# Constants on TensorE ahead of the first loads, the first pair in order of arrival, and the x casts and w_down sums at other places

## The chip, the cores and the metric

The kernel runs on one core of a Trainium2 chip. The time is the device time of one execution in microseconds (us), given as the median of several executions. Stage times inside an execution come from the trace of one profiled execution, counted from the start of its span; the span is about 2 us shorter than the device time (2303.0 for 2304.98 in before).

## The reference, cut to what matters

A gated MLP with 8 x 1024 tokens, hidden size 1024 and intermediate size 4096, all in float32:

```python
gate = x @ w_gate                      # x: (8, 1024, 1024), w_gate, w_up: (1024, 4096)
up = x @ w_up
gate = 0.5 * gate * (1 + np.tanh(np.sqrt(2 / np.pi) * (gate + 0.044715 * gate ** 3)))
h = gate * up
return (h @ w_down).astype(np.float32) # w_down: (4096, 1024)
```

## The kernel before

Eight passes of 1024 tokens. Each has a gate/up phase, which makes h, and a down phase, which multiplies h by w_down. All products are in float16 and use sums of blocks of the operands so that there are fewer products than blocks: seven for eight in passes 0 to 2. There one "pair" of 128-column blocks of gate and up takes 14 products of 4 matmuls; 16 pairs make a gate/up phase. Products are numbered 1 to 14 inside a pair, and other work is hung behind a product's number, which sets its place among the instructions of its engine.

Three inputs are prepared beside this. **x of the next pass** is cast to float16 by a transfer from DRAM to DRAM that GpSimd issues (`cast_x`), and then transposed by four transfers in the sync engine's queue (`transpose_x`). **Raw weights** come by casting loads that GpSimd issues (`load_raw`), and VectorE makes their sums (`sum_w`). **w_down** is loaded in pass 0 in four blocks, summed by VectorE and stored (`wd_load`, `wd_sums`, `wd_store`); the down phases read it back in chunks (`load_d`).

```python
def cast_x(p):
    r = slice(p * TOK, (p + 1) * TOK)
    nc.gpsimd.dma_start(out=xh[r, :], in_=x2[r, :])
...
# pass 0, block n of w_down: (distance from product s0, what, arguments)
s0 = 28 * n + 59
for ds, f, a in (
    (0, wd_load, (n, 0)), (2, wd_load, (n, 1)),
    (4, wd_load, (n, 2)), (6, wd_load, (n, 3)),
    (16, wd_sums, (0,)), (17, wd_sums, (1,)),
    (18, wd_sums, (2,)), (19, wd_sums, (3,)), (21, wd_store, (n,)),
):
    pr, k = divmod(s0 + ds - 1, 14)
    if pr == i:
        at(k + 1, f, *a)
...
if i == 4 and p == FAST - 1:           # FAST = 3: x of pass 3 in pair 4 of pass 2
    at(2, cast_x, p + 1)
...
# down phase, first product group
if v == 0 and p < FAST - 1:            # x of passes 1 and 2
    cast_x(p + 1)
if v == (2 if p < FAST - 1 else 0):
    transpose_x(p + 1)
```

In a pair from the third on, the ends of the products are used like this. "add s2 0" frees a PSUM bank, and in the next pair the ScalarE copies of the first product's sum ("copy 0", "copy 1") stand behind the gelu of that sum:

```python
AFTER1 = {
    1: ["copy 0"],                     # ScalarE: PSUM bank to PSUM bank
    2: ["copy 1"],
    ...
    11: ["h21"],                       # VectorE: up times gelu(gate)
    12: ["h11"],
    13: ["add s2 0"],                  # VectorE; its gelu is issued after product 1 of the next pair
    14: ["add s2 1"],
}
```

The first pair is special: x and the first weights come in pieces, and x is transposed on TensorE.

```python
def first_pair():                      # shortened
    for g in range(G): x0_cast(0, g)                   # VectorE, waits for the loads of x
    for g in range(G): x0_transpose(0, g)              # 8 transposes, one copy each by VectorE and ScalarE
    for kh in range(2):
        for w in range(2): cast_first(w, kh, slice(0, 256))    # ScalarE
    for kh in range(2): products(0, kh, slice(0, MH))  # 32 matmuls of 512 columns
    for g in range(2): x0_cast(1, g)
    for g in range(2): x0_transpose(1, g)
    outputs(0, 0); outputs(0, 1)                       # gelu and product
    for g in range(2, G): x0_cast(1, g)
    for kh in range(2): products(1, kh, slice(0, MQ))  # 32 of 256 columns
    for g in range(2, G): x0_transpose(1, g)
    for n, (kh, w) in enumerate(((0, 0), (0, 1), (1, 0), (1, 1))):
        cast_first(w, kh, slice(256, 512))
        if n == 1:                                     # trigger: waits for this cast
            nc.gpsimd.tensor_copy(mark, raw(0, 0)[:, w, kh * KH, 256:257])
            load_raw(0, 1)                             # second block of weights
    for kh in range(2): products(1, kh, slice(MQ, MH))
    ...
```

Of the kernel before, what the change touches and what calls it, by code (L numbers as in the profile page):

```python
# [14 lines left out]
GELU = mybir.ActivationFunctionType.Gelu_apprx_tanh  # L15
# [84 lines left out]
def kernel(  # L100
# [8 lines left out]
    nc = tc.nc  # L109
    x2 = x.flatten_outer_dims()  # L110
    out2 = out.flatten_outer_dims()
    P = 128
# [4 lines left out]
    MH = 512  # L117
# [6 lines left out]
    G = MH // P  # L124
# [94 lines left out]
    def x0_cast(mh, g):  # L219
        nc.vector.tensor_scalar(x0_f16[:, mh * G + g], x0_f32[mh][:, g], XSC, None, MUL)  # L220

    def x0_transpose(mh, g):
        h = x0_f16[:, mh * G + g]
        b = ps_free.popleft()
        ps = ps_all[:, b].bitcast(FP16).rearrange("p (k m) -> p k m", m=P)
        for k in range(2 * KH):
            nc.tensor.transpose(ps[:, k], h[:, k * P : (k + 1) * P], identity)
        c = slice(g * P, (g + 1) * P)
        nc.vector.tensor_copy(xq["b11" if mh == 0 else "b12"][:, :, c], ps[:, 0:KH])
        nc.scalar.copy(xq["b21" if mh == 0 else "b22"][:, :, c], ps[:, KH : 2 * KH])  # L230
        ps_free.append(b)


    def raw(p, q):
# [292 lines left out]
    def gate_up_one(p):  # L527
        for i in range(NP):
            q, e = divmod(i, 2)
            extra = {k: [] for k in range(1, 15)}  # L530

            def at(k, f, *a):
                extra[k].append(lambda: f(*a))

            if p == 0 and i == 0:
                first_pair()
                continue
            if p == 0:
                if e == 1:
                    at(13, load_raw, p, q + 2)  # L540
                if 11 <= i < 15:
                    at(7, half_load, 0, 2 * (i - 11))
                if i >= 14:
                    at(4, half_load, 1, 4 * (i - 14))
                    at(6, half_load, 1, 4 * (i - 14) + 2)
                for n in range(4):

                    s0 = 28 * n + 59
                    for ds, f, a in (
                        (0, wd_load, (n, 0)), (2, wd_load, (n, 1)),  # L550
                        (4, wd_load, (n, 2)), (6, wd_load, (n, 3)),
                        (16, wd_sums, (0,)), (17, wd_sums, (1,)),
                        (18, wd_sums, (2,)), (19, wd_sums, (3,)), (21, wd_store, (n,)),
                    ):
                        pr, k = divmod(s0 + ds - 1, 14)
                        if pr == i:
                            at(k + 1, f, *a)
            elif i == 0:
                at(1, load_raw, p, 1)
            elif e == 1:  # L560

                at(13, load_raw, p, q + 2)

            ks = (3, 5, 7, 9) if e == 0 else (11, 12, 13, 14)
            for n, k in enumerate(ks):
                at(k, sum_w, p, i + 1, n)

            if FAST - 2 <= p < FAST:
                for j, n in enumerate(entries_of(p - FAST + 2)):
                    if j // 6 == e:  # L570
                        at(2 * (j % 6) + 2, make_entry, p, q, n)
            if i == 4 and p == FAST - 1:
                at(2, cast_x, p + 1)
            if i == NP - 2:
                order[0] = [0, 1, 4, 2, 3, 5] if p % 2 == 0 else [2, 3, 4, 0, 1, 5]
                if p:
                    at(2, load_d, p, 0)
                    at(3, load_d, p, 1)
            if i == NP - 1:
                at(1, load_d, p, 2 if p else 0)  # L580
            second = p == 0 and i == 1
            pair(p, i, extra, SEQ0 if second else SEQ, AFTER0 if second else AFTER1)
# [134 lines left out]
    def down(p):  # L717
# [65 lines left out]
        for v, name in enumerate(DSEQ):  # L783
# [3 lines left out]
            for nb in range(2):  # L787
                kc = 2 * v + nb
                dc = d_chunk(p, kc)
                for g in range(G):  # L790
# [43 lines left out]
                            f()  # L834
                    if nb == 0 and g == 0 and p + 1 < NPASS:

                        if v == 0 and p < FAST - 1:
                            cast_x(p + 1)
                        if v == (2 if p < FAST - 1 else 0):
                            transpose_x(p + 1)  # L840
# [29 lines left out]


    def first_pair():
        bank = {}

        def products(mh, kh, c):
            for w in range(2):
                for j in range(2):
                    for k in range(KH):
                        nc.tensor.matmul(  # L879
                            ps_all[:, bank[mh, j, w], c],  # L880
                            raw(0, 0)[:, w, kh * KH + k, j * P : (j + 1) * P],
                            xq[f"b{kh + 1}{mh + 1}"][:, k, c],
                            start=(kh == 0 and k == 0 and c.start == 0),
                            stop=(kh == 1 and k == KH - 1),
                            skip_group_check=True,
                        )

        def outputs(mh, j):
            t = tmp_free.popleft()
            g, u = bank[mh, j, 0], bank[mh, j, 1]  # L890
            nc.scalar.activation(tmp[:, t], ps_all[:, g], GELU, scale=GSC)
            nc.vector.tensor_tensor(
                hq[f"a{mh + 1}{j + 1}"][:, 0, :], ps_all[:, u], tmp[:, t], MUL
            )
            tmp_free.append(t)
            ps_free.extend((g, u))

        def take(mh):
            for j in range(2):
                for w in range(2):  # L900
                    bank[mh, j, w] = ps_free.popleft()

        for g in range(G):
            x0_cast(0, g)
        for g in range(G):
            x0_transpose(0, g)
        for kh in range(2):
            for w in range(2):
                cast_first(w, kh, slice(0, 256))
        take(0)  # L910
        for kh in range(2):
            products(0, kh, slice(0, MH))
        for g in range(2):
            x0_cast(1, g)
        for g in range(2):
            x0_transpose(1, g)
        outputs(0, 0)
        outputs(0, 1)
        for g in range(2, G):
            x0_cast(1, g)  # L920
        take(1)
        for kh in range(2):
            products(1, kh, slice(0, MQ))
        for g in range(2, G):
            x0_transpose(1, g)

        b = list(ps_free)
        ps_free.clear()
        ps_free.extend((b[2], b[0], b[3], b[1]))
        for n, (kh, w) in enumerate(((0, 0), (0, 1), (1, 0), (1, 1))):  # L930
            cast_first(w, kh, slice(256, 512))
            if n == 1:

                nc.gpsimd.tensor_copy(mark, raw(0, 0)[:, w, kh * KH, 256:257])
                load_raw(0, 1)
        for kh in range(2):
            products(1, kh, slice(MQ, MH))
        sum_x(1)
        sum_w(0, 1, 0)
        sum_w(0, 1, 1)  # L940
        sum_x(2)
        outputs(1, 0)
        outputs(1, 1)
        sum_x(3)
        sum_w(0, 1, 2)
        sum_w(0, 1, 3)
        sum_x(4)
# [46 lines left out]
```

## Time and profile before

| | us |
|---|---|
| time before, median of 3 (lowest to highest) | 2301.93 (2298.45 to 2304.24) |
| start until the second pair's first product | 33.53 |
| pass 0, gate/up from there | 187.11 |
| pass 0, down | 102.47 |
| pass 1, gate/up and down | 194.13 and 96.69 |
| pass 2, gate/up | 196.81 |
| everything after that | 1492.26 |

These stages are read off TensorE's timeline of the profiled execution (span 2303.0): a stage begins where its first product starts. A down phase with no wait takes 96.69; pass 0's takes 5.78 more. 15 pairs of 12.09 us are 181.4; pass 0 takes 5.8 more. What the start, the three gate/up phases and that down phase have above their matmuls at full clock is what a change like this one can win.

The chain of work that ended last says the same in one line, as shares of the span by engine: most of the chain is TensorE itself, and some 8% goes through transfers and VectorE.

```profile
PE 90%; DMA 5%; DVE 3%; issue 1%; ACT 1%; POOL 0%; SPq 0%; POOLq 0%; DVEq 0%; ACTq 0%
```

Three stretches of 3.4 us, the time that the clock stayed at half after it fell (294.70 to 298.11): the two ahead of the place where TensorE's clock rose (18.22), and the one ahead of the place where it fell. The columns are the stretch, its length, then for TensorE matmuls, TensorE loads, VectorE, ScalarE and GpSimd the busy us and the count, then the granted clock, the DMA share and GB/s (the clock reads 1.00 in the first two lines too, ahead of the trace's first record of a change; there the count of matmuls, 14 in 5.80 us, shows the half clock):

```profile
11.40:14.80 3.40, 2.42 (x6) 0.88 (x7) 0.00 (x0) 3.32 (x4) 0.00 (x0) 1.00 1.10 375
14.80:18.20 3.40, 3.40 (x9) 1.21 (x8) 1.39 (x2) 0.53 (x1) 0.00 (x0) 1.00 1.02 408
291.30:294.70 3.40, 0.89 (x5) 0.45 (x6) 2.34 (x4) 0.00 (x0) 0.00 (x0) 1.00 1.01 357
```

Behind the first stretch, with 2.42 us of matmuls, the next is still slow: 9 matmuls in 3.40 us. After the second, in which TensorE was busy for all 3.40 us, they run at 216 ns. In the third, which holds most of the long wait, TensorE was busy for 0.89 us, and the following 3.4 us ran at half clock.

### The profile page before, as it was taken

The page shows a single profiled execution, that of the slowest core. Times are in us where ns is not written, and L with a number is a line of the kernel's source. Part 1 is how long each engine was busy: PE and PEld are TensorE (multiplying, and loading weights), DVE is VectorE, ACT ScalarE, POOL GpSimd, SP SyncE. Part 2 cuts the span into 40 slices and gives each one's busy share as a digit, 9 for nine tenths or more (in the row PEclk, how much of TensorE's full clock was granted, in tenths as well). Part 3 has the DMA queues.
Part 4 walks back from the last instruction along what each step waited for, and adds up shares of the span by engine and source line. Part 5 has one row for each costly group of instructions (what it writes and reads, how often), then busy time and mean ns, then how long its engine had stood idle before and what let it go on. Part 6 is the DMA issues. An engine that isn't in the chain of part 4 may idle for free.

```text
span 2303.0 us, 38141 instructions
## 1 busy us (share of the span) xinstructions
PE 2277.2 (99%) x14696; PEld 1436.5 (62%) x14696; DVE 1348.0 (59%) x1945; ACT 958.4 (42%) x1860; POOL 670.1 (29%) x818
## 2 busy tenths in 40 slices
PE   7999999999999999999999999999999999999999
PEld 4444444444444445888468874788747886488854
DVE  5566348873487753667446673476734667256650
ACT  4444125551255512555135551355414653055520
POOL 1333003320133300545014540254403543034520
PEclk9999999999999999999999999999999999999999
DMA  8898968989799876988679885798858988588852
GB/s 213 148 214 191 232 199 203 222 240 287 177 213 232 239 262 227 289 305 278 200 257 308 287 269 199 261 318 277 269 197 269 311 283 265 187 280 279 269 213 109
DMA packets 258054, 557.20 MB, mean 242 GB/s; under 512 B 74768, under 2 KB 134160, under 8 KB 243728
## 3 DMA queue, kind: packets, MB, share of 16 engines
q1 hardware_dynamic: 204992, 483.46, 62.4%
q0 software_dynamic: 52880, 71.31, 18.8%
q8 instruction: 115, 1.88, 0.3%
q14 instruction: 67, 0.55, 0.1%
HBM read 512.75 MB, written 113.25 MB: 272 GB/s over the span
## 4 chain that ended last, share of the span: by engine, by line
PE 90%; DMA 5%; DVE 3%; issue 1%; ACT 1%; POOL 0%; SPq 0%; POOLq 0%; DVEq 0%; ACTq 0%
PE ps L683 39%; PE ps L795 33%; PE ps L476 17%; DMA ring<-in_w_up_dram 2%; DMA h_s<-in_w_down_dram 2%; DVE ring L275 1%; DVE tmp L495 1%; DMA ring<-wd_ops 0%; PE ps L879 0%; DMA w_ops<-x_sums 0%; DVE h_a L513 0%; DMA h_a<-in_x_dram 0%; DVE x_sums L201 0%; POOL h_s L318 0%; ACT ring L253 0%
## 5 line engine op out<-in xcount | busy, mean ns | idle before, releaser
L683 PEld LDWEIGHTS <-ring 128*128 128x128 f16 x8320 | 813.7, 98 | 95.6
L660 POOL TENSOR_TENSOR h_a<-tmp 128x256 f16<-128x256 f32 x640 | 464.5, 745 | 928.3 <-ACT tmp L648 894.4
L683 PE MATMUL ps<-x_sums,ring 128*128 128x256 f16 x5760 | 655.8, 273 | 0.0
L795 PE MATMUL ps<-ring,h_a 128*128 128x512 f16 x2944 | 640.0, 380 | 3.9 <-DMA ring<-wd_ops 3.9
L645 DVE TENSOR_TENSOR tmp<-tmp,ps 128x512 f32<-128x512 f32 x640 | 413.7, 683 | 220.6 <-PE ps L683 167.8
L795 PEld LDWEIGHTS <-h_a 128*128 128x128 f16 x3072 | 300.7, 98 | 367.0 <-DVE x_b L183 4.4
L476 PEld LDWEIGHTS <-ring 128*128 128x128 f16 x2632 | 257.0, 98 | 320.8 <-issue 9.9
L630 ACT COPY tmp<-ps 128x512 f32<-128x512 f32 x520 | 304.1, 585 | 204.2 <-PE ps L683 121.9
L476 PE MATMUL ps<-x_sums,ring 128*128 128x512 f16 x1504 | 341.4, 379 | 7.5 <-DVE tmp L495 7.1
L648 ACT ACTIVATE tmp<-tmp 128x256 f32<-128x256 f32 x640 | 263.7, 417 | 173.0 <-DVE tmp L643 80.2
L734 ACT ACTIVATE tmp<-ps 128x512 f32<-128x512 f32 x128 | 76.4, 597 | 593.0 <-PE ps L795 591.9
L683 PE MATMUL ps<-x_b,ring 128*128 128x256 f16 x2560 | 305.6, 273 | 0.0
L476 PE MATMUL ps<-x_b,ring 128*128 128x512 f16 x1128 | 259.5, 379 | 0.5 <-ACT ps L492 0.5
L502 POOL TENSOR_TENSOR h_a<-tmp 128x512 f16<-128x512 f32 x94 | 145.3, 1546 | 382.6 <-ACT tmp L500 270.8
L643 DVE TENSOR_TENSOR tmp<-ps,tmp 128x512 f32<-128x512 f32 x240 | 165.3, 689 | 151.3 <-ACT tmp L630 105.2
L738 DVE SCALAR_TENSOR_TENSOR tmp<-ps,tmp 128x512 f32<-128x512 f32 x64 | 44.2, 690 | 309.2 <-ACT tmp L734 260.3
L495 DVE TENSOR_TENSOR tmp<-ps,tmp 128x512 f32<-128x512 f32 x188 | 126.9, 682 | 109.8 <-ACT tmp L487 106.8
L487 ACT COPY tmp<-ps 128x512 f32<-128x512 f32 x188 | 109.9, 585 | 91.7 <-PE ps L476 87.7
L742 DVE TENSOR_TENSOR h_a<-h_a,h_a 128x2048 f16<-128x2048 f16 x96 | 111.2, 1214 | 58.6 <-PE ps L795 58.6
L275 DVE TENSOR_TENSOR ring<-ring 128x1024 f16<-128x1024 f16 x188 | 135.0, 733 | 15.8 <-DMA ring<-in_w_up_dram 8.5
L500 ACT ACTIVATE tmp<-tmp 128x512 f32<-128x512 f32 x94 | 58.9, 626 | 153.4 <-DVE tmp L495 153.2
L795 PE MATMUL ps<-ring,h_s 128*128 128x512 f16 x480 | 104.9, 379 | 0.0
(65 smaller groups left out, 798.6 us busy)
## 6 DMA issues: line engine op xcount, KB each, us to landing
ring<-w_ops SPq DMA_DIRECT2D x480, 512.0 KB, 4.6
ring<-wd_ops SPq DMA_DIRECT2D x105, 1024.0 KB, 5.2
out_dram<-tmp SPq DMA_DIRECT2D x128, 256.0 KB, 2.5
w_ops<-x_sums SPq DMA_DIRECT2D x110, 256.0 KB, 6.5
ring<-in_w_gate_dram POOLq DMA_DIRECT2D x23, 1024.0 KB, 9.9
ring<-in_w_up_dram POOLq DMA_DIRECT2D x23, 1024.0 KB, 18.4
w_ops<-h_s SPq DMA_DIRECT2D x82, 256.0 KB, 5.5
x_half<-in_x_dram POOLq DMA_DIRECT2D x7, 2048.0 KB, 15.4
```

Of the source, the lines that this page charges most:

```text
L275: nc.vector.tensor_tensor(o, a, b, op)
L476: nc.tensor.matmul(ps(b, w), lhs[:, k], rhs[:, k, :], start=(first and k == 0), stop=(k == KH - 1), skip_group_check=True,)
L495: nc.vector.tensor_tensor(o, ps("b", w), o, ADD)
L502: nc.gpsimd.tensor_tensor(hq[TO[n]][:, i, :], tmp[:, t[n, 1]], tmp[:, t[n, 0]], MUL)
L630: nc.scalar.copy(tmp[:, t[o[1]]], ps_all[:, bank[o[2]]])
L643: nc.vector.tensor_tensor(d, b, a, SUB)
L645: nc.vector.tensor_tensor(d, a, b, ADD if o[4] == "add" else SUB)
L648: nc.scalar.activation(d, d, GELU, scale=GSC)
L660: nc.gpsimd.tensor_tensor(h, tmp[:, t[o[1]], MQ : 2 * MQ], g, MUL)
L683: nc.tensor.matmul(ps_all[:, bank[c], w * MQ : (w + 1) * MQ], lhs[:, w, k], rhs[:, k], start=(first and w == 0 and k == 0), stop=(k == KH ...
L742: nc.vector.tensor_tensor(hq[o][:, s, :], hq[a][:, s, :], hq[b][:, s, :], op)
L795: nc.tensor.matmul(ps_all[:, bank[b, g]], lhs[:, j, g * P : (g + 1) * P], dc[:, n, :], start=(first and j == 0), stop=(j == NP - 1), skip_ ...
```

## The change

Six things, none of which takes a product away:

- a. TensorE multiplies constants until the first products, and the gelu table is loaded at the start.
- b. The first pair's casts, gelus and products are issued in the order in which their inputs arrive.
- c. The second block of weights is loaded as soon as the second of the last four pieces of the first has come, not after ScalarE has cast that piece.
- d. The w_down sums of pass 0 stand 5 products later, and the store 4.
- e. x of pass 1 is cast in pair 2 of pass 0's gate/up phase, not in its down phase.
- f. x of pass 3 is cast in pair 13 of pass 2, not in pair 4.

```diff
-                        (16, wd_sums, (0,)), (17, wd_sums, (1,)),
-                        (18, wd_sums, (2,)), (19, wd_sums, (3,)), (21, wd_store, (n,)),
+                        (21, wd_sums, (0,)), (22, wd_sums, (1,)),
+                        (23, wd_sums, (2,)), (24, wd_sums, (3,)), (25, wd_store, (n,)),
...
-            if i == 4 and p == FAST - 1:
-                at(2, cast_x, p + 1)
+            if (p, i) in ((0, 2), (FAST - 1, 13)):
+                at(8, cast_x, p + 1)
...
-                        if v == 0 and p < FAST - 1:
+                        if v == 0 and 0 < p < FAST - 1:
                             cast_x(p + 1)
...
+        def warm(n):
+            for _ in range(n):
+                nc.tensor.matmul(ps_all[:, 0], warm_w, warm_x, start=True, stop=True)
+
+        warm_w, warm_x = hf["s3"][:, 0:P], hf["s3"][:, P : P + MH]
+        nc.vector.memset(hf["s3"][:, 0 : P + MH], 1.0)
+        nc.scalar.activation(mark, hf["s3"][:, 0:1], GELU)
         for g in range(G):
             x0_cast(0, g)
+        warm(9)
         for g in range(G):
-            x0_transpose(0, g)
+            x0_transpose(0, g, 4 + g)
+            warm(2 if g < G - 1 else 8)
...
         for g in range(2):
-            x0_transpose(1, g)
-        outputs(0, 0)
-        outputs(0, 1)
+            x0_transpose(1, g, 6 + g)
         for g in range(2, G):
             x0_cast(1, g)
-        take(1)
+        outputs(0, 0)
+        for w in range(2):
+            cast_first(w, 0, slice(256, 512))
+        nc.gpsimd.tensor_copy(mark, staging0(1, 0)[:, 0, 256:257])
+        load_raw(0, 1)
         for kh in range(2):
             products(1, kh, slice(0, MQ))
         for g in range(2, G):
-            x0_transpose(1, g)
-        ... (the four casts with the trigger behind the second)
+            x0_transpose(1, g, g - 2)
+        outputs(0, 1)
+        for w in range(2):
+            cast_first(w, 1, slice(256, 512))
         for kh in range(2):
             products(1, kh, slice(MQ, MH))
... (the banks of the first pair are given by number, no longer from the list of free ones)
```

Line numbers fall by one or two: L476, L495 and L275 of before are L474, L493 and L273 of the changed kernel, L879 is L877.

More of the change, by code (lines that the diff above doesn't have):

```diff
@@ L220, in x0_cast, with x0_transpose @@
         nc.vector.tensor_scalar(x0_f16[:, mh * G + g], x0_f32[mh][:, g], XSC, None, MUL)
-    def x0_transpose(mh, g):
+    def x0_transpose(mh, g, b):
         h = x0_f16[:, mh * G + g]
-        b = ps_free.popleft()
         ps = ps_all[:, b].bitcast(FP16).rearrange("p (k m) -> p k m", m=P)
@@ L230, in x0_transpose @@
         nc.scalar.copy(xq["b21" if mh == 0 else "b22"][:, :, c], ps[:, KH : 2 * KH])
-        ps_free.append(b)
     def raw(p, q):
@@ L872, in first_pair @@
     def first_pair():
-        bank = {}
+        bank = {(mh, j, w): 4 * mh + 2 * j + w for mh in range(2) for j in range(2) for w in range(2)}
         def products(mh, kh, c):
@@ L895, in outputs @@
             tmp_free.append(t)
-            ps_free.extend((g, u))
-        def take(mh):
-            for j in range(2):
-                for w in range(2):
-                    bank[mh, j, w] = ps_free.popleft()
+        def warm(n):
[4 more added lines that the diff above has]
+        nc.scalar.activation(mark, hf["s3"][:, 0:1], GELU)
         for g in range(G):
             x0_cast(0, g)
+        warm(9)
         for g in range(G):
-            x0_transpose(0, g)
+            x0_transpose(0, g, 4 + g)
+            warm(2 if g < G - 1 else 8)
         for kh in range(2):
@@ L909, in first_pair @@
                 cast_first(w, kh, slice(0, 256))
-        take(0)
         for kh in range(2):
@@ L924, in first_pair @@
         for g in range(2, G):
-            x0_transpose(1, g)
-        b = list(ps_free)
-        ps_free.clear()
-        ps_free.extend((b[2], b[0], b[3], b[1]))
-        for n, (kh, w) in enumerate(((0, 0), (0, 1), (1, 0), (1, 1))):
-            cast_first(w, kh, slice(256, 512))
-            if n == 1:
-                nc.gpsimd.tensor_copy(mark, raw(0, 0)[:, w, kh * KH, 256:257])
-                load_raw(0, 1)
+            x0_transpose(1, g, g - 2)
+        outputs(0, 1)
+        for w in range(2):
+            cast_first(w, 1, slice(256, 512))
         for kh in range(2):
             products(1, kh, slice(MQ, MH))
+        ps_free.clear()
+        ps_free.extend((0, 2, 1, 3, 4, 5, 6, 7))
         sum_x(1)
```

## The prediction

> **What bounds the kernel now.** I read the page's busy line first, then the list of waits for TensorE, then TensorE's timeline for each of those waits, last the transfers that stand behind them.
>
> ```profile
> PE 2277.2 (99%) x14696; PEld 1436.5 (62%) x14696; DVE 1348.0 (59%) x1945; ACT 958.4 (42%) x1860; POOL 670.1 (29%) x818
> ...
> PE ps L476 <- DVE tmp L495: 7.1, 5, 2.4
> PE ps L227 <- DVE h_a L220: 6.8, 5, 5.1
> PE ps L795 <- DMA ring<-wd_ops: 3.9, 1, 3.9
> PE ps L879 <- ACT ring L253: 2.3, 1, 2.3
> PE ps L879 <- DVE x_b L229: 1.1, 2, 0.6
> PE ps L476 <- ACT ps L492: 0.5, 1, 0.5
> ```
>
> TensorE is the bound: all its waits (us in total, times, longest) make 21.7 us. A 512-column matmul starts every 216 ns when it runs freely (100 of L476 in 21.60 us), so a pair of pass 0 to 2 (56 of them) costs 12.09 us; nothing in the change takes real matmuls away. It can only win the waits and any matmuls that ran slowly. These lie in the first 51 us, in pass 0 and once in pass 2 (TensorE's timeline, idle time and its releaser in brackets):
>
> ```profile
> 12.38 9.95 PE L879 MATMUL ps<-x_b,ring 128*128 128x512 f16 x32 [2.32 <-ACT ring L253]
> 22.16 1.06 PE L227 MATMUL ps<-identity,h_a 128*128 128x128 f16 x16
> 23.81 3.65 PE L879 MATMUL ps<-x_b,ring 128*128 128x256 f16 x32 [0.59 <-DVE x_b L229]
> 28.31 1.22 PE L227 MATMUL ps<-identity,h_a 128*128 128x128 f16 x16 [0.85 <-DVE h_a L220]
> 30.04 3.65 PE L879 MATMUL ps<-x_b,ring 128*128 128x256 f16 x32 [0.52 <-DVE x_b L229]
> ...
> 50.97 4.48 PE L476 MATMUL ps<-x_sums,ring 128*128 128x512 f16 x20 [1.92 <-DVE tmp L495]
> 149.26 4.48 PE L476 MATMUL ps<-x_sums,ring 128*128 128x512 f16 x20 [1.26 <-DVE tmp L495]
> 174.89 4.48 PE L476 MATMUL ps<-x_sums,ring 128*128 128x512 f16 x20 [1.29 <-DVE tmp L495]
> 293.81 22.56 PE L795 MATMUL ps<-ring,h_a 128*128 128x512 f16 x96 [3.93 <-DMA ring<-wd_ops]
> 374.43 4.48 PE L476 MATMUL ps<-x_sums,ring 128*128 128x512 f16 x20 [0.21 <-DVE tmp L495]
> 716.59 4.48 PE L476 MATMUL ps<-x_sums,ring 128*128 128x512 f16 x20 [2.44 <-DVE tmp L495]
> ```
>
> The slow matmuls show in the windows: 14 in the first 5.80 us, 19 in the next 3.80 us, and again half the clock just after the wait at 293.81:
>
> ```profile
> 12.40:18.20 5.80, 5.80 (x14) 2.07 (x15) 1.39 (x2) 2.85 (x3) 0.00 (x0) 1.00 1.05 399
> 18.30:22.10 3.80, 3.80 (x19) 1.74 (x18) 0.00 (x0) 0.00 (x0) 0.00 (x0) 1.00 1.07 350
> ...
> 294.70:298.10 3.40, 3.40 (x10) 0.50 1.06 425
> ```
>
> (The column of the granted clock says 1.00 in the first line; the count of matmuls says half.) The wait of 3.93 us comes from the sync engine's queue: its four transposes of x sat there for 30.89 us and held back the w_down chunk behind them.
>
> ```profile
> 250.59 30.89 SPq L178 DMA_TRANSPOSE x_b<-x_half  x4
> 281.52 0.60 SPq L379 DMA_DIRECT2D wd_ops<-ring  x1
> 282.21 0.61 SPq L379 DMA_DIRECT2D wd_ops<-x_sums  x1
> 282.93 1.38 SPq L398 DMA_DIRECT2D ring<-wd_ops  x1
> ```
>
> [...]TensorE starts at half clock[...]: 427 ns, then 216 ns from 18.2 us on, and 0.50 after 3.93 us idle. [...]L275 takes 1.37 instead of 0.68 us at 144.89, beside a GpSimd product from 144.45 to 145.72.
>
> **The change part by part.**
>
> *a. Matmuls on constants.* Nine of 427 ns (3.84 us) run from about 1.2 us, as soon as VectorE has set the constants, until the first x cast at about 5.1; then 2, 2, 2 and 8 between and after the transposes. They take no real work's place if the clock rises by about 8 us: warm, the last eight need 8 x 0.216 = 1.73 us from about 9.6, done at 11.3. The first real product stays at 12.38, because ScalarE still ends its four copies of x and the first weight cast only then. From there 5.84 us at 427 ns become 13.7 matmuls at 216 ns: **2.9 us** won.
>
> *b. Order of the first pair.* After the first 32 products (now to 19.3) the two transposes and the copies take what they took. The wait of 0.85 goes: the casts of the last x rows now stand before the gelu product in VectorE's order, so they are done at about 22.2, before TensorE needs them at 24.4. The gelu table is loaded at the start, 1.28 us off ScalarE, which was not TensorE's wait itself. The second pair starts at 33.43 - 2.9 - 0.85, about 29.6; its wait of 0.49 for ScalarE's copies shrinks to about 0.05, because ScalarE casts half the weights before the last x copies and ends them at about 29.1. Won: **1.3 us**.
>
> *c. Second block of weights sooner.* GpSimd now issues it when the first block's second half of w_up arrives (landed at 22.41), not after ScalarE's cast at 32.56. With the 8.9 and 12.9 us it took from issue to landing it lands at about 31.5 and 36.5. VectorE's sums need it at about 29.6 + 11 x 0.86 = 39. Before, it landed at 46.59, the sums waited 2.36 us and TensorE **1.92 us**. That goes.
>
> *d. w_down sums 5 products (4.3 us) later.* They no longer wait for loads that landed at 141.0 and 166.6. But now three of each four stand before "add s2 0", in a stretch where VectorE is full from 94.41 (block 0's times). The first fits in the gap of 1.02 us; the other two, 0.60 us apart each, push that add from 96.81 to 98.03. In block 2 TensorE went on 1.88 us after the start of that add (147.38 to 149.26: add, gelu, bank copy). So 99.91, where it would go on at 99.32: a wait of 0.6 us, in all four blocks, 2.4 us, against 1.26 + 1.29 = 2.55 before. **About 0**.
>
> *e. x of pass 1 cast in pair 2.* In the down phase this transfer (15.4 us to landing, from 223.7) delayed the stores of w_down before the transposes, and the block of gate weights issued at 241.83, which landed at 261.0 (19.2 us). Without it that block should land by about 251 and the last store by about 253, so the transposes start on free queues. The up weights, issued at 255.64, still collide with the last two. I expect the queue free at about 276 instead of 281.5, the chunk issued at about 277 and landed at about 287, before TensorE needs it at 289.9. Won: 3.93, plus 3.41 us at half clock, **1.7 us**: 5.6. At its new place the transfer falls into 55 to 66 us; before, no DMA runs from 60 to 70, so it costs nothing there.
>
> *f. x of pass 3 cast in pair 13.* In pair 4 it was issued at 666.83 and landed at 690.72; weights issued at 685.5 landed at 712.2, and the sums held TensorE **2.44 us**. In pair 13 no weight loads of this pass follow. It is issued some 29 us before the down phase and lands, even at 24 us, before the transposes.
>
> Sum: 2.9 + 1.3 + 1.9 + 0 + 5.6 + 2.4 = 14.1 us; 2301.9 - 14.1 = 2287.8.
>
> **Rivals.** *R1, the clock does not rise in time.* If transposes do not count as activity, the mixed stretch is only half busy; for scale, in before the 3.4 us up to 14.8 held 2.4 us of matmuls and did not release it[...]. Then TensorE is still slow at 11, the eight constants end at 14.5 instead of 11.3 and delay the first product: a gives about 0, the time is about 2291. [...]I give it 15%. *R2, the transposes stay slow anyway.* They ran at 125 to 138 ns a packet from 260 to 272 us, when the weights' load was beside them, and at 20 ns from 278 on; that load remains. Then the chunk is still late, e gives 0 to 3, and the time is about 2291 to 2293. I give it 20%. *R3, VectorE is fuller than counted* in d: [...]four blocks, up to 3 us lost. *R4, the moved transfers make new waits*, at 55 to 85 us for the first w_down block or at the start of pass 2's down phase (stores and chunks in the same 29 us): 1 to 4 us, 10%. *R5, d wins its 2.5 us whole*, if I have the banks' order wrong: 2285.
>
> **Range and chances.** Weighted with R1 and R2 the 14.1 fall to about 13.3: I predict 2288.5 us. All rivals together give 2296, the best case 2284; run to run, before spread over 5.8 us. Range 2283 to 2295. 2% is 46 us, twice all of TensorE's waits: faster 0.01, within 2% 0.985, slower 0.005.
>
> **What would show it.** a: 32 products in 7.1 us from 12.4. b, c: the second pair starts near 29.6 and no wait before 45 us is over 0.7. d: four waits of about 0.6 for L493 (old L495); none, or over 1, is a miss. e: no wait in pass 0's down phase and no half clock after it; transposes done by 270. f: no wait in pass 2. The prediction is wrong if the gain is under 8 us (then R1 and R2 both hold) or over 18 us (then time lay in something I took for fixed).

## The result, and the profile after

| | before, us | after, us |
|---|---|---|
| median of 4 (lowest to highest) | 2301.36 (2298.45 to 2304.24) | 2288.87 (2288.21 to 2291.30) |
| profiled execution, span | 2303.0 | 2287.4 |
| start until the second pair | 33.53 | 29.48 |
| pass 0, gate/up from there | 187.11 | 183.92 |
| pass 0, down | 102.47 | 96.69 |
| pass 1, gate/up | 194.13 | 194.85 |
| pass 1, down | 96.69 | 96.69 |
| pass 2, gate/up | 196.81 | 193.50 |
| everything after that | 1492.26 | 1492.27 |

The ratio is 0.9948, with a 95% interval of 0.9930 to 0.9965: faster, but within 2%. (A ratio is the mean time of one kernel's runs over that of the other's of the same rounds, so it isn't quite the ratio of the medians.) The stages add up: 4.05 + 3.19 + 5.78 - 0.72 + 3.31 = 15.61, and the spans differ by 15.6. The medians differ by less, 12.5. The profiled execution of before is a slow one among its own kind: its device time was 2304.98, above the four in the table.

TensorE is now busy for practically the whole span, the constants included, as the page's busy line and the chain that ended last say:

```profile
PE 2276.5 (100%) x14719; PEld 1437.7 (63%) x14719; DVE 1342.2 (59%) x1946; ACT 958.6 (42%) x1860; POOL 676.4 (30%) x818
...
PE 97%; DVE 2%; issue 0%; DMA 0%; ACT 0%; SPq 0%; DVEq 0%; ACTq 0%
```

The 23 more matmuls are the constants. The share of transfers in the chain has gone from 5% to 0%. The two largest of what remains of TensorE's waits (us in total, times, longest):

```profile
PE ps L474 <- DVE ring L273: 2.0, 4, 0.7
PE ps L898 <- DVE h_s L901: 1.6, 1, 1.6
```

The wait for a transfer (3.9 in before) is not there. The first line is new; the second is the start, before VectorE has set the constants. TensorE's timeline of the first 30 us (start, us, instruction, idle time before it and its releaser):

```profile
1.59 4.02 PE L898 MATMUL ps<-h_s 128*128 128x512 f16 x9 [1.59 <-DVE h_s L901]
...
9.47 1.89 PE L898 MATMUL ps<-h_s 128*128 128x512 f16 x8
12.37 7.08 PE L877 MATMUL ps<-x_b,ring 128*128 128x512 f16 x32 [1.01 <-ACT ring L251]
...
29.48 3.63 PE L474 MATMUL ps<-x_b,ring 128*128 128x512 f16 x16
```

Nine constants take 4.02 us, so about 430 ns each at first; the eight at 9.47 take 1.89. The first real product starts where it did before (12.38), but the 32 of it take 7.08 us instead of 9.95. The stretches on both sides agree: the clock rises at 5.7, after 3.40 us in which TensorE was busy for all 3.40, mostly with constants (11 matmuls in the first line, 32 shorter ones in the second). How much of that it takes isn't shown.

```profile
2.30:5.70 3.40, 3.40 (x11) 1.30 (x10) 0.73 (x2) 0.00 (x0) 0.00 (x0) 1.00 0.95 366
5.70:9.10 3.40, 2.91 (x32) 1.62 (x30) 2.19 (x4) 0.00 (x0) 0.00 (x0) 1.00 1.03 394
```

In pass 0 TensorE now waits once for each block of w_down, always before the third product of a pair (0.42, 0.42, 0.70 and 0.42 us; the first is shown); and once more in pass 1:

```profile
93.10 4.48 PE L474 MATMUL ps<-x_sums,ring 128*128 128x512 f16 x20 [0.42 <-DVE ring L273]
...
422.88 4.48 PE L474 MATMUL ps<-x_sums,ring 128*128 128x512 f16 x20 [0.86 <-ACT ps L490]
```

The view puts the first down to a sum of weights. VectorE's timeline, then ScalarE's, ahead of the wait at 93.10 give the chain:

```profile
90.02 0.68 DVE L336 TENSOR_TENSOR h_s<-h_s 128x1024 f16<-128x1024 f16 x1
...
91.22 0.68 DVE L493 TENSOR_TENSOR tmp<-ps,tmp 128x512 f32<-128x512 f32 x1
```

```profile
91.94 0.63 ACT L498 ACTIVATE tmp<-tmp 128x512 f32<-128x512 f32 x1 [4.46 <-DVE tmp L493]
92.47 1.06 ACT L490 COPY ps<-ps 128x512 f32<-128x512 f32 x2
```

(The list counts idle time from the modelled end of the matmul before, 379 ns after its start by the page's mean, while matmuls that nothing held up started 216 ns apart, 100 in 21.60 us. So each wait is 0.16 us longer from start to start: here 0.58.)

L336 is the third w_down sum. "add s2 0" (L493) follows at 91.22, its gelu at 91.94, the two bank copies from 92.47; the first of them ends at about 93.05, and TensorE goes on at 93.10. So the wait ends with ScalarE's copy, 1.88 us after the start of the add, and the releaser named in the bracket was only the last event that the profile could match. The two w_down sums before the add (L334 at 88.22, and L336) made it late: it starts 3.61 us after the product of h21 (87.61), and in before, without them, 2.40 us after it (94.41 and 96.81).

The sync engine's queue in pass 0's down phase:

```profile
242.77 19.75 SPq L178 DMA_TRANSPOSE x_b<-x_half  x4
...
263.98 1.44 SPq L396 DMA_DIRECT2D ring<-wd_ops  x1
```

The four transposes hold it for 19.75 us, not 30.89. The chunk that TensorE waited for is issued at 263.98 and landed at 274.87, 7.8 us before its product at about 282.6. Why the queue is faster shows in the transfers of 205 to 290 us, by kind (destination and source, queue, operation, count, KB each, median us from issue to landing). In the kernel before:

```profile
x_half<-in_x_dram POOLq DMA_DIRECT2D x1, 2048.0 KB, 15.4
...
ring<-in_w_gate_dram POOLq DMA_DIRECT2D x1, 1024.0 KB, 19.2
ring<-in_w_up_dram POOLq DMA_DIRECT2D x1, 1024.0 KB, 22.2
x_b<-x_half SPq DMA_TRANSPOSE x4, 12.3
```

And in the changed kernel:

```profile
ring<-in_w_gate_dram POOLq DMA_DIRECT2D x1, 1024.0 KB, 11.1
ring<-in_w_up_dram POOLq DMA_DIRECT2D x1, 1024.0 KB, 10.1
x_b<-x_half SPq DMA_TRANSPOSE x4, 8.0
```

Without the cast of x, both weight loads take about half as long. How that quickens the transposes is not shown. It isn't only that fewer loads lie beside them: by the times of the single transfers, the second transpose holds the queue for 6.07 us (248.89 to 254.96) although the up weights' load (248.40 to 258.48) lies beside all of it.

### The profile page after: what moved, and what is told of

The parts are those of the page before. It is cut to its first block, busy times and chain, and to the rows that moved or that the text cites. A ratio compares the mean times of both kernels' runs of the same rounds, so it can differ in the third digit from the quotient of the medians.

```text
span 2287.4 us, 38185 instructions
## 1 busy us (share of the span) xinstructions
PE 2276.5 (100%) x14719; PEld 1437.7 (63%) x14719; DVE 1342.2 (59%) x1946; ACT 958.6 (42%) x1860; POOL 676.4 (30%) x818
## 3 DMA queue, kind: packets, MB, share of 16 engines
q8 instruction: 115, 1.88, 0.4%
## 4 chain that ended last, share of the span: by engine, by line
PE 97%; DVE 2%; issue 0%; DMA 0%; ACT 0%; SPq 0%; DVEq 0%; ACTq 0%
PE ps L681 40%; PE ps L793 34%; PE ps L474 23%; PE ps L877 1%; DVE ring L273 1%; DVE tmp L493 0%; DMA h_a<-in_x_dram 0%; DVE h_a L511 0%; DVE x_sums L201 0%; DVE h_s L334 0%; DVE h_s L336 0%; DVE h_s L338 0%; ACT x_b L229 0%; DVE x_b L228 0%; SPq L217 0%
## 5 line engine op out<-in xcount | busy, mean ns | idle before, releaser
L474 PEld LDWEIGHTS <-ring 128*128 128x128 f16 x2632 | 257.5, 98 | 314.5 <-issue 4.7
L474 PE MATMUL ps<-x_sums,ring 128*128 128x512 f16 x1504 | 341.0, 379 | 3.0 <-DVE ring L273 2.0
L500 POOL TENSOR_TENSOR h_a<-tmp 128x512 f16<-128x512 f32 x94 | 150.4, 1600 | 375.1 <-ACT tmp L498 286.1
L474 PE MATMUL ps<-x_b,ring 128*128 128x512 f16 x1128 | 259.1, 379 | 0.0
L493 DVE TENSOR_TENSOR tmp<-ps,tmp 128x512 f32<-128x512 f32 x188 | 127.0, 683 | 137.5 <-ACT tmp L485 134.6
L273 DVE TENSOR_TENSOR ring<-ring 128x1024 f16<-128x1024 f16 x188 | 132.7, 721 | 6.9 <-PE ps L793 3.8
```

What stands on the lines that cost most here:

```text
L273: nc.vector.tensor_tensor(o, a, b, op)
L474: nc.tensor.matmul(ps(b, w), lhs[:, k], rhs[:, k, :], start=(first and k == 0), stop=(k == KH - 1), skip_group_check=True,)
L493: nc.vector.tensor_tensor(o, ps("b", w), o, ADD)
L500: nc.gpsimd.tensor_tensor(hq[TO[n]][:, i, :], tmp[:, t[n, 1]], tmp[:, t[n, 0]], MUL)
```

## The experiments

Twelve runs. Unless something else is said, a diff is against the changed kernel. Three groups ran on one chip each beside runs of before: the first four (before: 2299.79), the next four (2301.57) and the last four (2300.54; these are four of the first group's seven executions). Timed runs are all in the fast state; a run without rounds is a single one, so its state is unknown and I compare its stages, not its time.

### Without the constants

```diff
-            for _ in range(n):
+            for _ in range(0):
                 nc.tensor.matmul(ps_all[:, 0], warm_w, warm_x, start=True, stop=True)
```

> The changed kernel with no matmuls on constants, all else kept. My theory: the first 32 products start at 12.4 us as before but run about 13 of them at 427 ns, so they take about 9.9 us instead of 7.08, the second pair starts near 32.4 instead of 29.5, and the time is 2.5 to 3.0 us longer than the changed kernel's. The rival, that the new order of the first pair carries that stage, expects under 1 us.

Measured: 2292.22 us (2291.14 to 2292.87), ratio to before 0.9968 (0.9953 to 0.9983).

```profile
12.30 9.20 PE L877 MATMUL ps<-x_b,ring 128*128 128x512 f16 x32 [2.32 <-ACT ring L251]
...
31.53 3.63 PE L474 MATMUL ps<-x_b,ring 128*128 128x512 f16 x16
```

The first product starts as before at 12.30, and its 32 matmuls are slow again. The constants are worth 31.53 - 29.48 = 2.05 us here, less than the 2.87 between before and after, because the clock rose at 16.6 in this run and at 18.2 in before; why it does so at different times isn't shown. The gain is confirmed; its size varies.

### x of pass 1 cast in the down phase again

```diff
-            if (p, i) in ((0, 2), (FAST - 1, 13)):
+            if (p, i) == (FAST - 1, 13):
...
-                        if v == 0 and 0 < p < FAST - 1:
+                        if v == 0 and p < FAST - 1:
```

> The changed kernel with x of pass 1 cast at the start of pass 0's down phase again. My theory: the four transposes take some 30 us on the sync engine's queue again instead of 20, a w_down chunk comes 3 to 4 us late, half clock follows for 3.4 us, and the down phase of pass 0 takes about 102.3 us instead of 96.7: the time is 5 to 6 us longer. The rival, that the wait came from the stores of w_down and the load of up weights alone, expects a down phase under 98 us.

Measured: 2295.04 us (2289.93 to 2296.82), ratio 0.9977 (0.9961 to 0.9993). The down phase took 101.62 instead of 96.69. The sync queue, then TensorE after its wait, then the transfers by kind:

```profile
244.72 29.55 SPq L178 DMA_TRANSPOSE x_b<-x_half  x4
...
275.72 1.34 SPq L396 DMA_DIRECT2D ring<-wd_ops  x1
```

```profile
286.81 15.47 PE L793 MATMUL ps<-ring,h_a 128*128 128x512 f16 x64 [3.26 <-DVE x_b L183]
```

```profile
ring<-in_w_gate_dram POOLq DMA_DIRECT2D x1, 1024.0 KB, 19.9
ring<-in_w_up_dram POOLq DMA_DIRECT2D x1, 1024.0 KB, 21.4
x_b<-x_half SPq DMA_TRANSPOSE x4, 11.4
```

One transfer put back, and the weight loads take twice as long, the transposes hold the queue for 29.55 us, the chunk is issued 11.7 us later, 0.9 of that because the phase began later (it landed at 286.67, and TensorE went on at 286.81, whatever the bracket names), and the matmuls behind the wait are slow at first: 64 of them took 15.47 us, 1.5 more than at 216 ns from start to start. 3.26 + 0.16 + 1.5 = 4.92, and the phase is 4.93 longer. So putting the cast back is enough to bring the loss back.

It takes more than the cast, though. Pass 1's down phase begins with the same cast in both kernels (16.2 us to landing in the changed one), and there the four transposes hold the queue for only 14.9 us and TensorE waits nowhere: 96.69 us. It has no w_down sums to store, and its gate weights are issued only at 574.47, long after the transposes. Which of these the cast needs beside it was not tested, and the way from one to the other stays open: in this run the cast had landed at 233.03, before the gate weights were issued (235.50), and yet the second transpose took 11.61 us beside the up weights, for 6.07 without the cast. Nor does it cost as much every time: one of the four timed runs took 2289.93 us, 1.1 over the changed kernel.

### x of pass 3 cast in pair 4 again

```diff
-            if (p, i) in ((0, 2), (FAST - 1, 13)):
+            if (p, i) == (0, 2):
                 at(8, cast_x, p + 1)
+            if i == 4 and p == FAST - 1:
+                at(2, cast_x, p + 1)
```

> The changed kernel with x of pass 3 cast in pair 4 of pass 2 again. My theory: one wait of about 2.4 us comes back in pass 2, whose gate and up phase takes 196.5 to 197 us instead of 193.5. The rival, that the wait in the kernel before was a matter of phase that the earlier changes have moved, expects under 194.5.

Measured: 2293.70 us (2292.32 to 2294.79), ratio 0.9974 (0.9960 to 0.9989).

```profile
704.97 4.48 PE L474 MATMUL ps<-x_sums,ring 128*128 128x512 f16 x20 [2.07 <-DVE tmp L493]
```

The wait is back, with 2.07 us, and pass 2's gate/up phase takes 196.51 instead of 193.50. Confirmed. The phase loses 0.94 more than the wait; I come back to that below. (Also, two loads of x landed 1.1 us later in this run and the first product started at 13.52. Nothing in the edit concerns them.)

### The w_down sums at their old place

```diff
-                        (21, wd_sums, (0,)), (22, wd_sums, (1,)),
-                        (23, wd_sums, (2,)), (24, wd_sums, (3,)), (25, wd_store, (n,)),
+                        (16, wd_sums, (0,)), (17, wd_sums, (1,)),
+                        (18, wd_sums, (2,)), (19, wd_sums, (3,)), (21, wd_store, (n,)),
```

> The changed kernel with the w_down sums at their old places. My theory: the four waits of 0.42, 0.42, 0.70, 0.42 us (together 1.96) go, and two of about 1.3 us come back, so the gate and up phase of pass 0 is 183.9 to 184.9 us long, against 183.9: no difference over 1 us. The rival, that the later sums are worth the 2.5 us that the old waits showed, expects 186.4.

Measured: 2287.22 us (2286.79 to 2287.89), ratio 0.9947 (0.9930 to 0.9963). Pass 0's gate/up phase took 181.32, with no wait for a sum at all. Both expectations missed: neither had the phase without any wait. Either the loads of w_down were faster once the other parts were in, or their landing varies from run to run. The next three runs were made to tell these apart.

### Before once more, with a profile

> The kernel before, unchanged, profiled a second time. Its first profile was the slowest of its runs (2305 us). If the two waits of about 1.3 us for the w_down loads and the 3.93 us for the w_down chunk are fixed by the program, they come back within 0.3 us. If they hang on how fast the transfers ran in that run, pass 0 is shorter here: waits of 0 to 0.6 us in the gate and up phase, and a wait for the chunk that is shorter by 1 us or more. I lean to the second for the w_down loads, because with the old places of the sums the changed kernel had no wait at all.

This is the kernel before, unedited. Measured: 2308.69 us in a single run, span 2306.8.

```profile
147.53 4.48 PE L476 MATMUL ps<-x_sums,ring 128*128 128x512 f16 x20 [1.06 <-DVE tmp L495]
173.38 4.48 PE L476 MATMUL ps<-x_sums,ring 128*128 128x512 f16 x20 [1.30 <-DVE tmp L495]
293.17 23.82 PE L795 MATMUL ps<-ring,h_a 128*128 128x512 f16 x96 [4.81 <-DMA ring<-wd_ops]
```

The waits for w_down in before are reproducible here: 1.06 and 1.30 for 1.26 and 1.29. The wait in the down phase was 4.81 us, and the clock was at half for 6.8 us after it; in pass 2 another 3.4 us at half clock followed its waits. So the same kernel loses 1.7 us to the clock in one profile and some 4.6 in the other (half of the time at half clock in which TensorE worked). I had leaned to a shorter run; that missed, the waits come back.

### The changed kernel once more

> The changed kernel, unchanged, beside the next two on the same chip: four waits of 0.4 to 0.7 us again in the gate and up phase of pass 0 (183.5 to 184 us), since they come from the order of VectorE's work and not from transfers.

Unedited too. Measured: 2289.02 us (2288.47 to 2289.39), ratio 0.9947 (0.9932 to 0.9962). Four waits of 0.42 us each, gate/up of pass 0 183.64. So the late sums cost nearly the same in both profiles of the changed kernel.

### The sums at their old place, once more

> The changed kernel with the w_down sums at their old places, on the same chip. It had no wait over 0.15 us in pass 0 (181.3 us). If that holds, the later sums cost 2 us and this one is 1.5 to 2.5 us faster than the changed kernel. If the missing waits were that run's fast transfers, one or two waits of up to 1.3 us come back and the two are equal.

The same kernel as the fourth run. Measured: 2287.37 us (2285.57 to 2288.81), ratio 0.9937 (0.9921 to 0.9954).

```profile
141.84 4.48 PE L474 MATMUL ps<-x_sums,ring 128*128 128x512 f16 x20 [0.82 <-DVE tmp L493]
167.28 4.48 PE L474 MATMUL ps<-x_sums,ring 128*128 128x512 f16 x20 [1.11 <-DVE tmp L493]
```

Now the waits are there: 0.82 + 1.11 = 1.93, and the phase took 183.57. With the sums at the old place it depends on when w_down lands (for block 2 VectorE's first sum, after waiting for the load, starts at 132.44 here and at 130.61 in the fourth run): no wait in one run, 1.93 us in another. At the new place the waits are 1.7 to 2.0 us in seven profiles, and 2.87 and 4.05 in two (the runs with x of pass 1 cast in the down phase and with the late trigger). Part d is thus no gain: the phase takes 183.6 to 183.9 us in most profiles with it, and 181.32 and 183.57 without it; on this chip the median without it is 1.65 us shorter, and three of its four runs are below all four of the changed kernel. What makes the loads land earlier or later I don't know.

### Loads and sums of w_down on even places

My reading was that the late sums cost something only because they stand before "add s2 0". So I put the loads 6 products later and spread the sums over the first half of the following pair, where no "add s2 0" stands behind them.

```diff
-                        (0, wd_load, (n, 0)), (2, wd_load, (n, 1)),
-                        (4, wd_load, (n, 2)), (6, wd_load, (n, 3)),
-                        (21, wd_sums, (0,)), (22, wd_sums, (1,)),
-                        (23, wd_sums, (2,)), (24, wd_sums, (3,)), (25, wd_store, (n,)),
+                        (6, wd_load, (n, 0)), (8, wd_load, (n, 1)),
+                        (10, wd_load, (n, 2)), (12, wd_load, (n, 3)),
+                        (26, wd_sums, (0,)), (28, wd_sums, (1,)),
+                        (30, wd_sums, (2,)), (32, wd_sums, (3,)), (34, wd_store, (n,)),
```

> The changed kernel with the w_down loads 6 products later and the sums 10 to 13 products after the old places, at products 1, 3, 5 and 7 of the next even pair, where VectorE has room before its next add. My theory, that only the place inside the pair makes the four waits and not the sums' own time: no wait over 0.2 us in pass 0, 181.3 to 181.8 us, whatever the transfers do. The rival, that four more sums in any pair delay VectorE's adds too much, expects waits of 0.4 us and more in the even pairs.

Measured: 2286.72 us (2286.52 to 2286.92), ratio 0.9937 (0.9922 to 0.9952): the best of all, 2.3 us under the changed kernel on the same chip. VectorE's timeline in block 0:

```profile
92.62 1.75 DVE L332 TENSOR_TENSOR h_s<-h_s 128x1024 f16<-128x1024 f16 x1
...
96.82 0.68 DVE L338 TENSOR_TENSOR h_s<-h_s 128x1024 f16<-128x1024 f16 x1
...
98.02 1.28 DVE L493 TENSOR_TENSOR tmp<-ps,tmp 128x512 f32<-128x512 f32 x2
```

The s2 adds (L493 ahead of these lines, the last at 91.42) come first, then all four sums, done at 97.5, and then the two s3 adds at 98.02, even though one sum took 1.75 us. From the second pair of pass 0 on TensorE waits nowhere in that pass for more than 0.15 us, and its gate/up phase took 181.31, which is 15 pairs of 12.09. The cost of part d is one of place, not of amount: VectorE does the same sums. (The loads were moved by 6 products too; the sums weren't moved alone.)

### Transposes instead of constant products

Do transposes alone raise the clock as products do? Each constant matmul is replaced by four transposes of a constant tile, about as long together.

```diff
-            for _ in range(n):
-                nc.tensor.matmul(ps_all[:, 0], warm_w, warm_x, start=True, stop=True)
+            ps = ps_all[:, 0].bitcast(FP16)
+            for k in range(4 * n):
+                nc.tensor.transpose(ps[:, 0:P], warm_w, identity)
```

> The changed kernel with each matmul on constants replaced by four transposes of a constant 128x128 tile (the same 427 ns at half clock), so TensorE does nothing but transposes until the first product. If transposes count as activity, the clock is full by about 8 us and the 32 products take 7.1 us. If they do not[...], the clock stays at half until 15 to 19 us and the products take 8.5 to 9.9 us. [...]I give the first 60%.

Measured: 2289.25 us, one run.

```profile
1.59 4.02 PE L899 MATMUL ps<-identity,h_s 128*128 128x128 f16 x36 [1.59 <-DVE h_s L902]
...
9.52 1.95 PE L899 MATMUL ps<-identity,h_s 128*128 128x128 f16 x32
12.42 7.08 PE L877 MATMUL ps<-x_b,ring 128*128 128x512 f16 x32 [0.95 <-ACT ring L251]
```

36 transposes took 4.02 us at the start, 32 took 1.95 us from 9.52 on, and the products are fast from their first on. Transposes raised the clock at the same 5.7 us as products did.

Transposes didn't raise it in every run. In the run without constants four groups of eight, with 0.22 to 0.27 us between them, were TensorE's only work from 5.12 to 9.99 us; each group took 1.03 to 1.04 us, at half clock to the last, and the clock rose at 16.6. Whether transposes count as products do, no run decides.

### Only the first nine constants

```diff
             x0_transpose(0, g, 4 + g)
-            warm(2 if g < G - 1 else 8)
```

> The changed kernel with the nine constants at the start and none between and after the transposes. If the sustained start is enough, the clock is full by 8 us and stays so[...]: 32 products in 7.1 us. If the mixed stretch is needed[...], the clock rises only at 15 to 19 us and the products take 8.5 to 9.9 us. I give each half.

Measured: 2291.58 us, one run.

```profile
6.60:10.00 3.40, 1.74 (x24) 1.23 (x22) 2.27 (x5) 0.52 (x2) 0.00 (x0) 1.00 1.04 378
10.00:13.40 3.40, 0.87 (x3) 0.32 (x4) 0.44 (x2) 3.40 (x7) 0.00 (x0) 0.51 1.11 352
```

The clock rose at 6.6, and fell again at 10.0, after 3.40 us in which TensorE was busy for 1.74, with transposes alone. It rose anew at 16.9. The 32 products took 9.2 us, and the second pair started at 31.77, later than without any constants. Nine constants, with the first transposes behind them, raised the clock (at 6.6 here) but didn't hold it; with the fourteen between and after the transposes it stayed up (the 32 products took 7.08 us). Neither expectation had that whole.

### The second block of weights triggered late

```diff
-        nc.gpsimd.tensor_copy(mark, staging0(1, 0)[:, 0, 256:257])
-        load_raw(0, 1)
         for kh in range(2):
             products(1, kh, slice(0, MQ))
...
             cast_first(w, 1, slice(256, 512))
+        nc.gpsimd.tensor_copy(mark, raw(0, 0)[:, 1, KH, 256:257])
+        load_raw(0, 1)
```

> The changed kernel with the second block of weights issued after ScalarE's last cast of the first block, near 29 us, instead of 24.5. My theory: it lands at about 42, three us after the sums need it (39), and TensorE waits 1.0 to 1.9 us in the second or third pair. The rival, that the new order alone removed the old wait of 1.92, expects none over 0.3.

Measured: 2296.39 us, one run. (The trigger waits for the last of the four casts here; in before it waited for the second.) The block landed at 38.66 and 43.69 instead of 32.96 and 38.0.

```profile
43.74 1.04 PE L474 MATMUL ps<-x_b,ring 128*128 128x512 f16 x4 [0.96 <-DMA ring<-in_w_up_dram]
...
48.08 6.13 PE L474 MATMUL ps<-x_sums,ring 128*128 128x512 f16 x20 [1.92 <-DVE tmp L493]
```

```profile
44.60:48.00 3.40, 1.20 (x5) 0.41 (x5) 3.40 (x7) 1.09 (x3) 0.00 (x0) 1.00 1.22 198
48.00:51.40 3.40, 3.32 (x8) 1.17 (x8) 3.37 (x5) 1.09 (x3) 2.12 (x2) 0.51 1.24 206
```

Three waits (the third, of 0.36 us, lies between these), 3.24 us together; then, behind a stretch in which TensorE was busy for 1.20 of 3.40 us, 3.4 us at half clock, 1.7 lost; and the waits for the w_down sums later in the pass grew from 1.96 to 4.05. That makes 7.0 of the 7.5 us by which the gate/up phase was longer (191.4 for 183.9); the 0.16 us that each of the three new waits is longer from start to start makes the rest. The direction was as expected, the size far over it: I had counted only a wait. It also shows that the order of the first pair (part b) alone would not have removed the wait of 1.92 us.

### The gelu table loaded where it was

```diff
-        nc.scalar.activation(mark, hf["s3"][:, 0:1], GELU)
```

> The changed kernel without the gelu on one constant column, so that the 1.28 us table load stands before the first real gelu again, near 21.4 us. My theory: ScalarE has room there, TensorE's first products and the second pair's start (29.5) move by under 0.2 us. The rival, that the early table load is part of the gain, expects the second pair 0.5 to 1.3 us later.

Measured: 2290.34 us, one run. The second pair starts at 29.43, for 29.48 with the early load. The table load is 1.28 us of ScalarE at 21.5 us (1.28 us at 24.44 in before), where nobody waits for it. As expected, no effect.

## Why the prediction was right

The predicted 2288.5 and the measured 2288.87 agree, and each term of the sum has the right sign in the profiles (d was put at 0). That the number fits so well is partly luck: in the profiles the terms come to 15.6 us where 14.1 were predicted, and the timed medians differ by 12.5. Point by point:

**a, constants.** Predicted 2.9; 9.95 - 7.08 = 2.87. The first product at 12.4 and its 7.1 us came as written. Nine, with the first transposes behind them, were enough to raise the clock (at 5.7 us here, at 6.6 in the run with nine alone), and that run shows that the prediction missed a point: nine would not have been enough, since there the clock fell again at 10.0, behind the stretch of transposes. Undone, a was worth 2.05 at the second pair.

**b, order.** Predicted 1.3. The wait of 0.85 is gone and the second pair starts at 29.48, predicted 29.6; 4.05 - 2.87 = 1.18 of that stage is b. The wait of 0.49 for ScalarE's copies, which lay in the second pair, is gone too: 1.67 in all. (The 33.43 in the prediction's sum is the start of a weight load; the matmul's is 33.53.) No run undid b alone, so its size is read from the stages.

**c, earlier block.** Predicted a gain of 1.9 by a block that lands at 31.5 and 36.5. It landed at 32.96 and 38.0, because the piece that triggers it came at 23.79 in this run (22.41 in before); still early enough. (The second load took 12.83 us in before, not 12.9.) The wait of 1.92 is gone. The late trigger shows that the term was sized as a mere wait: without c, but with the new order, that one run lost more than 7 us.

**d, sums later.** Predicted 4 x 0.6 = 2.4 lost for 2.55 won. The path (third sum, add, gelu, bank copy, 1.88 us from add to TensorE) is what the timelines show. So is the size. The list shows 0.42 + 0.42 + 0.70 + 0.42 = 1.96, but from start to start the first wait is 0.58 (92.52, where the third product would start, to 93.10), for 0.6 predicted: together some 2.6, and the phase is 2.6 longer than the 181.31 of the run without such waits. The other side of the term, that the old waits always cost 2.55, holds in the two profiles of before (2.55 and 2.36), but not with the other parts in: there the old place cost 0 and 1.93 in two runs. So "about 0" was right against before's profile, and against the same kernel with the old place it is a loss of up to 2.6.

**e, x of pass 1.** Predicted 5.6, measured 5.78: 3.93, the 0.16 that the list leaves out, and 1.69 at half clock. The steps hold, but I had the queue only at half of its gain: the transposes were free at 262.57. The changed kernel is 7.24 us ahead there (4.05 + 3.19), so this is 269.8 in before's time, where the prediction had 276; the check in its list ("done by 270") fits better than its own working. The weights' loads sped up twice over, from 19.2 and 22.2 to 11.1 and 10.1 us, and the one I had left to "still collide" lay beside the second and third transposes all the same, at 10.1. The prediction's reading, that the transposes are slow when the weights' load is beside them, is therefore not the whole of it. The term could not show this, since the wait and the slow clock were gone either way. At its new place the cast ran from 45.69 to 64.62, not 55 to 66, and so beside the third block of weights (41.60 to 54.94); no wait came of it.

**f, x of pass 3.** Predicted 2.44, measured 3.31, and 3.01 when it is undone. The wait accounts for 2.44 and 2.07, from start to start for 2.60 and 2.23; the rest, 0.7 to 0.8, is spread in hitches of some 0.1 us, none of which the list of waits names alone. Their sum varies: in the eleven profiles with f, none with a listed wait in pass 2, its gate/up phase takes 193.49 to 194.85 (16 pairs of 12.09 are 193.4). So up to 1.4 of a difference in this stage can be chance.

**Not foreseen.** Pass 1's gate/up phase lost 0.72. In the changed kernel TensorE waited 0.86 at 422.88, after a chain that starts with a 1.75 us sum of VectorE beside a GpSimd product:

```profile
417.46 1.27 POOL L500 TENSOR_TENSOR h_a<-tmp 128x512 f16<-128x512 f32 x1 [5.22 <-DVE tmp L493]
417.53 1.75 DVE L201 TENSOR_TENSOR x_sums<-ring,x_sums 128x1024 f16<-128x1024 f16 x1
```

A sum of the same line and size takes 0.68 at 420.40, with no GpSimd product beside it. The change needn't have made it: the second profile of before has waits of 0.90 and 0.33 with the same releaser named, and over all fourteen profiles this phase takes 194.13 to 195.86, before's two among them (194.13 and 195.06). So the 0.72 is within what varies by chance.

**The sum.** 4.05 (a, b) + 3.19 (the rest of b, c, d) + 5.78 (e) + 3.31 (f) - 0.72 = 15.61 in the profiles. The 3.19 are made of 0.49 + 1.92 + 2.55 - 1.96 = 3.00 and hitches. Of the rivals, R1 (slow clock), R2 (transposes still slow), R3 (VectorE fuller; one block waited 0.28 longer than the others) and R4 (new waits of the moved transfers) did not come; the weights that I gave them took 0.8 off, which brought the number closer to the timed median by luck. R5 (d wins whole) did not come either.

**What stays open.** The timed gain is smaller than the profiles' as far as the record shows because before varies and the changed kernel hardly does. For 14 timed runs of before the granted clock is on record: three with 1.000 average 2297.8 us, nine with 0.999 2300.7, two with 0.998 2304.9. All timed runs of the changed kernel have 1.000. That goes with 3.4 us at half clock after the start in one profile of before and 10.2 in the other; what decides it was not tested. Nor was it tested why the two profiled executions were among the slowest. Because before varies so, the medians of the parts undone (3.3, 6.2 and 4.8 us for a, e and f) don't add up to the whole: their sum, 14.3, is already above 12.5. How the cast of x slows the transfers after it in pass 0 stays open too.

## What to carry to other kernels

Where an engine is 99% busy, list its waits one by one, follow each to the transfer or the instruction that ended it, and add them up; a transfer that nobody waits for can still be the one to move, if it lies beside a chain of others that somebody does wait for. Look for slow matmuls behind waits of a few microseconds (here behind those of 3.26, 3.93 and 4.81 us and behind three of 3.24 together), because half clock cost nearly as much again as some of them (1.7 us behind a wait of 1.92). See after a warm-up that the clock stays up: with nine constants alone it fell again behind 3.40 us in which TensorE was busy for 1.74. Add a list's waits up from start to start, because idle time counted from a modelled end left out 0.16 us of each. If extra work must go onto an engine in a tuned schedule, its place counts more than its amount: the same sums cost 2.3 to 2.6 us before an instruction that frees a bank and nothing 5 to 8 products later still.
